# Turns of probabilities and value products, two key tiles at a time, in an attention phase on one core

## The chip, the core and the metric

The kernel runs on one core of a Trainium2 chip. The time is the device time of one execution in microseconds (us); of several runs the median is given. The core's engines run side by side, each through its own queue in program order: TensorE (PE; its weight loads are shown apart as PEld), VectorE (DVE), ScalarE (ACT), GpSimd (POOL) and SyncE (SP), which issues most of the DMAs. TensorE reads from SBUF and writes into PSUM, which is handed out here in banks of 128 partitions by 512 floats.

## The reference

One layer of a decoder: a sparse attention beside a state-space layer, then an output projection and a gated feed-forward network, for a prompt of 1024 rows and for eight short decode rows. The change is in the attention of the prompt. Its core, for one chunk of 128 queries:

```python
s_s = jnp.einsum('bqgrd,bqgkjd->bqgrkj', qg, k_sel)...      # selected blocks: all earlier keys here
p_s = masked_softmax(s_s * scale, key_pos <= q_pos)
o_s = jnp.einsum('bqgrn,bqgnd->bqgrd', p_s, v_sel)
p_w = masked_softmax(einsum(qg, kv_win[:, :, 0]) * scale, m_w)   # sliding window of 512
o_w = jnp.einsum('bqgrw,bwgd->bqgrd', p_w, kv_win[:, :, 1])
o = g[..., 0:1] * o_c + g[..., 1:2] * o_s + g[..., 2:3] * o_w
```

There are 8 query heads in 2 groups of 4; a group shares its keys and values, 64 wide. The top 16 blocks of 64 keys are all the blocks that a prompt of 1024 has, so the selected branch attends to all earlier keys.

## The kernel before

The program is recorded in Python and then ordered, engine by engine, by a scheduler that works with an estimate of times of its own; what it made is read from the order of instructions, shown below. It runs in phases: projection, decode rows with the compressed cache, prompt attention (`phase_attend`, with the state-space layer, the gating products and the second half of the decode attention put between its parts), output projection (`phase_mix`) and feed-forward.

Prompt attention takes query tiles of 128 rows in the order 4, 0, 6, 1, 7, 2, 5, 3 (`ORDER`). A tile c has two branches, `br` 0 over key tiles 0 to c and `br` 1 over at most five key tiles, and each is done in two halves `hf` of four heads. Such a half unit has two parts. `attend_scores` multiplies queries with keys into PSUM `as`, takes the maximum on VectorE and the exponential on ScalarE into `ap`, one strip of probabilities for each of four heads. `attend_values` follows one unit later (`LOOK`) and goes over the key tiles t. For each, `pv_tile` (line 1272) does three things:

- the turn: four transposes (line 1279), one for each head, of a block of 128 by 128 probabilities into one PSUM bank `pt`;
- the copy: the bank to SBUF, `pT`, alternately on ScalarE and VectorE (line 1281);
- the value product: two products (line 1283), one for each group, 64 columns of values by 256 of `pT`, adding into bank `aso`. The two write different halves of the partitions.

At the end `attend_out` copies `aso` away, transposes it and adds it to `att`. The compressed branch is done once for a query tile, with one key tile (`ac`, two steps).

The names in the trace: `as702pt` is the turn of query tile 7, branch 0, key tile 2; `as702pT` its copy; `aso<-as702pT` the product. The two halves share names. An f32 product stands as two rows of the trace, so a value product of one key tile is "x4" there and "x2" in the order.

PSUM has two banks for `pt` (`psum("psc", s=2, t=2, o=1, f=1)`, tag `t`, also used by `attend_out` and the turns of queries), one for `aso` (`o`) and two double ones for scores (`s`). `pT` has three buffers. Nothing but data, buffers and the scheduler's choice sets the order of turns and products. The helper `behind` (line 812), used in the decode part, makes the scheduler keep one instruction behind another on the same engine; it signals nothing.

Of the kernel before, what the change touches and what calls it, by code (L numbers as in the profile page):

```python
# [9 lines left out]
F32 = mybir.dt.float32  # L10
# [79 lines left out]
class Kernel:  # L90
# [1134 lines left out]
    def attend_values(self, c, br, hf, st, Ps, pc):  # L1225

        nc = self.nc
        k0, nk = self.attend_keys(c, br)
        if hf == 0:
            st["O"] = self.ps("o", f"aso{c}{br}")  # L1230
        O, att, l = st["O"], st["att"], st[br]
        g = self.gz[:, c].rearrange("p (h b) -> p b h", b=3)
        for t in range(nk):
            self.pv_tile([P[:, t * 128:t * 128 + 128] for P in Ps], self.vst[:, k0 + t, br, :], O, hf, pc, f"as{c}{br}{t}", t == 0, t == nk - 1)
        st["between"](2 * br + hf)
        if hf == 0:
            return
        nc.vector.reciprocal(l, l)
        nc.vector.tensor_tensor(l, l, g[:, 1 + br], op=ALU.mult)
        self.attend_out(O, l, att, pc, f"as{c}{br}", br == 0)  # L1240
        if br == 0:
            return
        O = self.ps("o", f"aco{c}")
        for i in range(2):
            self.pv_tile([st["pcb"][:, h, :] for h in (2 * i, 2 * i + 1, 4 + 2 * i, 5 + 2 * i)], self.vcp, O, i, pc, f"ac{c}", True, True)
        self.attend_out(O, st["lc"], att, pc, f"ac{c}", False)
        t = pc.tile([128, 512], F32, tag="aot", name=f"attq{c}")
        self.norm_rows(att.rearrange("p h d -> p (h d)"), t, 1.0, self.xc_d[c * 128:(c + 1) * 128, :512], f"attn{c}", "a")
# [20 lines left out]
            nc.vector.tensor_scalar(l, l, self.k("cmp_any"), None, op0=ALU.mult)  # L1269
        return l  # L1270

    def pv_tile(self, Ps, V, O, hf, pc, name, first, last):

        nc = self.nc
        n = Ps[0].shape[-1]
        pT = pc.tile([128, 512], F32, tag="apT", name=f"{name}pT{hf}", bufs=3)[:n]
        p = self.ps_t(f"{name}pt{hf}")[:n]
        for r in range(4):
            nc.tensor.transpose(p[:, r * 128:r * 128 + 128], Ps[r], self.ident)
        self.flip = not self.flip  # L1280
        (nc.scalar.copy if self.flip else nc.vector.tensor_copy)(pT, p)
        for g in range(2):
            nc.tensor.matmul(O[64 * g:64 * g + 64, 256 * hf:256 * hf + 256], V[:n, 64 * g:64 * g + 64], pT[:, 256 * g:256 * g + 256],  # L1283
                             start=first, stop=last)

    def attend_out(self, O, coef, att, pc, name, first):

# [618 lines left out]
```

## Time and profile before

| | us |
|---|---|
| median of 3 runs | 1836.43 (1834.63 to 1841.58) |
| the profiled execution | 1828.84 |
| its span | 1827.1 |
| TensorE busy | 1709.1 (94%) |
| TensorE's weight loads | 1439.4 (79%) |
| VectorE busy | 972.2 (53%) |
| ScalarE busy | 618.9 (34%) |
| GpSimd busy | 427.1 (23%) |

The span is the time from the first to the last instruction in the profile. Shares are averages over the phases. A row of the trace in order of time gives the start, the duration, the engine, the line and the operation; in square brackets stands how long the engine was idle ahead of it and what ended that. Durations of matmuls overlap, since they are pipelined: how long a piece really takes from TensorE is the distance from its start to the start of the next piece. The first turn of prompt attention starts at 477.3 us, the last value product at about 947 us.

### The profile page before, as it was taken

The numbers are of one execution on the slowest core, as the hardware profiler recorded it, in microseconds if no ns is written. First come the engines' busy times: TensorE is split into PE (matmuls) and PEld (weight loads), VectorE is DVE, ScalarE is ACT, GpSimd is POOL, SyncE is SP. The second block draws the span as 40 slices with busy tenths as digits, with TensorE's granted clock in tenths as the row PEclk, the third lists the DMA queues.
The fourth block names the chain that finished last, engine by engine and source line by source line (L and its number), as shares of the span: only waits on it lengthen the run. The fifth ranks groups of instructions, "written<-read, shape, count | busy, mean of one in ns | idle before, by whom it ended". The sixth has DMA issues, their size and how long they took to land.

```text
span 1827.1 us, 29355 instructions
## 1 busy us (share of the span) xinstructions
PE 1709.1 (94%) x11546; PEld 1439.4 (79%) x11546; DVE 972.2 (53%) x2330; ACT 618.9 (34%) x1247; POOL 427.1 (23%) x817
## 2 busy tenths in 40 slices
PE   6998999899796899999989989999999999999997
PEld 3898988788564665655657888998998999999996
DVE  4867647588988466566535443323333333333346
ACT  4523146455453355565433341111111111211210
POOL 2344545232015313341122210110110110110150
PEclk9999999899898999999999999999999999999999
DMA  8333243645231345413114221101201201201113
GB/s 297 105 86 106 70 152 119 219 157 193 65 112 63 71 161 195 152 61 104 55 60 138 92 93 58 58 24 50 67 24 47 70 24 47 70 24 47 53 47 141
DMA packets 132699, 172.43 MB, mean 94 GB/s; under 512 B 17176, under 2 KB 92312, under 8 KB 132304
## 3 DMA queue, kind: packets, MB, share of 16 engines
q1 hardware_dynamic: 123024, 136.62, 23.4%
q0 software_dynamic: 9408, 33.89, 5.8%
q8 instruction: 91, 1.49, 0.3%
q14 instruction: 48, 0.39, 0.1%
q10 hardware_dynamic: 128, 0.04, 0.0%
HBM read 143.88 MB, written 25.46 MB: 93 GB/s over the span
## 4 chain that ended last, share of the span: by engine, by line
PE 61%; DVE 6%; DMA 4%; ACT 2%; issue 1%; POOL 1%; SPq 1%; DVEq 0%; ACTq 0%; POOLq 0%
PE gu L1810 19%; PE dn L1853 13%; PE g L1810 5%; PE u L1810 4%; PE aso L1283 3%; PE as L1205 1%; PE as L1206 1%; SPq L1596 1%; PE acs L1258 1%; PE mx8M L1728 1%; PE mx2M L1728 1%; PE mx5M L1728 1%; PE mx0M L1728 1%; PE mx1M L1728 1%; PE mx4M L1728 1%
## 5 line engine op out<-in xcount | busy, mean ns | idle before, releaser
L1810 PE MATMUL gu<-h2h,wh 128*128 128x352 f32 x704 | 227.8, 324 | 5.0 <-ACT h2h L870 5.0
L1810 PE MATMUL gu<-h2h,wl 128*128 128x352 f32 x704 | 227.3, 323 | 0.0
L1810 PE MATMUL gu<-h2l,wh 128*128 128x352 f32 x704 | 226.8, 322 | 0.0
L1859 DVE TENSOR_TENSOR acc<-acc,dn 128x512 f32<-128x512 f32 x144 | 98.9, 687 | 229.9 <-PE dn L1853 229.9
L1818 POOL TENSOR_TENSOR al<-fa,ah 128x352 fp32r<-128x352 f32 (+1 forms) x66 | 69.6, 1054 | 414.8 <-ACT ah L1817 408.8
L1813 ACT ACTIVATE fa<-gu 128x352 f32<-128x352 f32 x44 | 20.4, 465 | 412.1 <-PE gu L1810 412.1
L1853 PE MATMUL dn<-dh,ah 128*128 128x512 f32 x352 | 140.3, 399 | 5.6 <-DVE fin L1862 5.2
L1810 PEld LDWEIGHTS gu<-h2h,wh 128*128 128x128 f32 x704 | 132.5, 188 | 7.9 <-ACT h2h L870 5.3
L1853 PE MATMUL dn<-dl,ah 128*128 128x512 f32 x352 | 138.7, 394 | 0.0
L1853 PE MATMUL dn<-dh,al 128*128 128x512 f32 x352 | 138.3, 393 | 0.0
L1810 PEld LDWEIGHTS gu<-h2l,wh 128*128 128x128 f32 x704 | 133.0, 189 | 3.8
L1810 PEld LDWEIGHTS gu<-h2h,wl 128*128 128x128 f32 x704 | 132.7, 188 | 3.1
L1816 DVE TENSOR_TENSOR fa<-fa,gu 128x352 f32<-128x352 f32 x44 | 22.9, 521 | 143.0 <-ACT fa L1813 143.0
L409 ACT CAST wh<-wr 128x1024 fp32r<-128x1024 f32 x44 | 46.0, 1048 | 151.8 <-PE g L1810 77.0
L1205 PE MATMUL as<-kst,aqA 128*128 128x320 f32 (+4 forms) x192 | 76.7, 403 | 16.2 <-ACT ap L1222 9.3
L1853 PEld LDWEIGHTS dn<-dh,ah 128*128 128x128 f32 x352 | 66.1, 188 | 24.5 <-ACT wh L409 7.5
L410 DVE TENSOR_TENSOR wl<-wr,wh 128x1024 fp32r<-128x1024 f32 x44 | 58.8, 1339 | 49.3 <-ACT wh L409 49.3
L1853 PEld LDWEIGHTS dn<-dl,ah 128*128 128x128 f32 x352 | 66.1, 188 | 15.6
L1853 PEld LDWEIGHTS dn<-dh,al 128*128 128x128 f32 x352 | 66.3, 188 | 8.1
L1222 ACT ACTIVATE ap<-as,asm 128x640 f32<-128x640 f32 (+3 forms) x64 | 55.8, 873 | 46.6 <-DVE asm L1221 31.3
L1221 DVE TENSOR_REDUCE asm<-as 128x1 f32<-128x640 f32 (+3 forms) x64 | 58.5, 918 | 20.7 <-PE as L1209 19.8
L1206 PE MATMUL as<-kst,aqB 128*128 128x320 f32 (+4 forms) x192 | 65.1, 344 | 4.7 <-ACT aqB L1168 4.7
(2137 smaller groups left out, 4667.9 us busy)
## 6 DMA issues: line engine op xcount, KB each, us to landing
wada<-in_w_ada SPq DMA_DIRECT2D x24, 1024.0 KB
wr<-in_w_ffn_gate SPq DMA_DIRECT2D x22, 512.0 KB
wr<-in_w_ffn_up SPq DMA_DIRECT2D x22, 512.0 KB
wd<-in_w_ffn_down SPq DMA_DIRECT2D x22, 512.0 KB
bx<-in_x_prompt SPq DMA_DIRECT2D x8, 512.0 KB
s_raw<-in_cache_kv_win SPq DMA_DIRECT2D x8, 512.0 KB
wor<-in_w_out SPq DMA_DIRECT2D x16, 256.0 KB
ex<-x_d SPq DMA_DIRECT2D x8, 512.0 KB
```

Of the source, the lines that this page charges most:

```text
L409: self.nc.scalar.copy(hi, raw)
L410: self.nc.vector.tensor_tensor(lo, raw, hi.bitcast(F32), op=ALU.subtract)
L1205: nc.tensor.matmul(Sv, qA[:, h, :], kk, start=True, stop=False)
L1206: nc.tensor.matmul(Sv, qB[:, h, :], kk, start=False, stop=not mt)
L1221: nc.vector.tensor_reduce(mx[:, :1], Sv, axis=ax, op=ALU.max, negate=True)
L1222: nc.scalar.activation(Pv, Sv, AF.Exp, bias=mx[:, :1], accum_out=l[:, h:h + 1])
L1283: nc.tensor.matmul(O[64 * g:64 * g + 64, 256 * hf:256 * hf + 256], V[:n, 64 * g:64 * g + 64], pT[:, 256 * g:256 * g + 256], start=first, s ...
L1728: nc.tensor.matmul(M[:P, :], X[k][b], w[:, k, c], start=m == 0, stop=m == 23)
L1810: nc.tensor.matmul(gu[i], w[:, k, :], h[:, k, 352 * n:352 * n + 352], start=m == 0, stop=m == 23)
L1818: nc.gpsimd.tensor_tensor(al[:, cols], a[:, :w], ah[:, cols].bitcast(F32), op=ALU.subtract)
L1853: nc.tensor.matmul(p, a[:, sl], w[:, c], start=m == 0, stop=m == 5)
L1859: nc.vector.tensor_tensor(o, o, p, op=ALU.add)
```

## The change

`pv_tile` becomes `pv_tiles`, which gets all key tiles of a half unit. It goes over them in groups of two. It records the turns (and copies) of a group, then the products of the group before; after the last group its products follow. With `behind`, every turn's first transpose is held behind the last instruction of the piece before it in this row, and every product likewise, so that the scheduler keeps the row: turns 0 and 1, turns 2 and 3, products 0 and 1, turns 4 and 5, products 2 and 3, and so on. Other work may still be put between. `pT` gets a fourth buffer. The compressed branch calls the new function with one key tile, twice. Everything else is the same text.

```diff
@@ -1230,8 +1230,8 @@
             st["O"] = self.ps("o", f"aso{c}{br}")
         O, att, l = st["O"], st["att"], st[br]
         g = self.gz[:, c].rearrange("p (h b) -> p b h", b=3)
-        for t in range(nk):
-            self.pv_tile([P[:, t * 128:t * 128 + 128] for P in Ps], self.vst[:, k0 + t, br, :], O, hf, pc, f"as{c}{br}{t}", t == 0, t == nk - 1)
+        self.pv_tiles([([P[:, t * 128:t * 128 + 128] for P in Ps], self.vst[:, k0 + t, br, :], f"as{c}{br}{t}", t == 0, t == nk - 1)
+                       for t in range(nk)], O, hf, pc)
         st["between"](2 * br + hf)
         if hf == 0:
             return
@@ -1242,7 +1242,7 @@
             return
         O = self.ps("o", f"aco{c}")
         for i in range(2):
-            self.pv_tile([st["pcb"][:, h, :] for h in (2 * i, 2 * i + 1, 4 + 2 * i, 5 + 2 * i)], self.vcp, O, i, pc, f"ac{c}", True, True)
+            self.pv_tiles([([st["pcb"][:, h, :] for h in (2 * i, 2 * i + 1, 4 + 2 * i, 5 + 2 * i)], self.vcp, f"ac{c}", True, True)], O, i, pc)
         self.attend_out(O, st["lc"], att, pc, f"ac{c}", False)
         t = pc.tile([128, 512], F32, tag="aot", name=f"attq{c}")
         self.norm_rows(att.rearrange("p h d -> p (h d)"), t, 1.0, self.xc_d[c * 128:(c + 1) * 128, :512], f"attn{c}", "a")
@@ -1269,19 +1269,42 @@
             nc.vector.tensor_scalar(l, l, self.k("cmp_any"), None, op0=ALU.mult)
         return l
 
-    def pv_tile(self, Ps, V, O, hf, pc, name, first, last):
-
-        nc = self.nc
+    def pv_tiles(self, tiles, O, hf, pc):
+
+
+        groups = [tiles[i:i + 2] for i in range(0, len(tiles), 2)]
+        prev, wait = None, []
+        for grp in groups + [None]:
+            if grp:
+                turned = []
+                for tile in grp:
+                    pT, ins = self.pv_turn(tile, hf, pc)
+                    prev = self.behind(prev, ins[0])
+                    prev = ins[-1]
+                    turned.append((tile, pT))
+                wait.append(turned)
+            if len(wait) > (1 if grp else 0):
+                for tile, pT in wait.pop(0):
+                    ins = self.pv_product(tile, pT, O, hf)
+                    self.behind(prev, ins[0])
+                    prev = ins[-1]
+
+    def pv_turn(self, tile, hf, pc):
+        nc = self.nc
+        Ps, _, name, _, _ = tile
         n = Ps[0].shape[-1]
-        pT = pc.tile([128, 512], F32, tag="apT", name=f"{name}pT{hf}", bufs=3)[:n]
+        pT = pc.tile([128, 512], F32, tag="apT", name=f"{name}pT{hf}", bufs=4)[:n]
         p = self.ps_t(f"{name}pt{hf}")[:n]
-        for r in range(4):
-            nc.tensor.transpose(p[:, r * 128:r * 128 + 128], Ps[r], self.ident)
+        ins = [nc.tensor.transpose(p[:, r * 128:r * 128 + 128], Ps[r], self.ident) for r in range(4)]
         self.flip = not self.flip
         (nc.scalar.copy if self.flip else nc.vector.tensor_copy)(pT, p)
-        for g in range(2):
-            nc.tensor.matmul(O[64 * g:64 * g + 64, 256 * hf:256 * hf + 256], V[:n, 64 * g:64 * g + 64], pT[:, 256 * g:256 * g + 256],
-                             start=first, stop=last)
+        return pT, ins
+
+    def pv_product(self, tile, pT, O, hf):
+        _, V, _, first, last = tile
+        n = pT.shape[0]
+        return [self.nc.tensor.matmul(O[64 * g:64 * g + 64, 256 * hf:256 * hf + 256], V[:n, 64 * g:64 * g + 64], pT[:, 256 * g:256 * g + 256],
+                                      start=first, stop=last) for g in range(2)]
 
     def attend_out(self, O, coef, att, pc, name, first):
```

The order of instructions on TensorE, at two places. In its rows a number behind `ap` stands for one strip of probabilities, one behind `pt` for one turn, and one behind `aso` for one branch of a query tile, both halves of it.

Query tile 7, branch 0, first half, in the middle of its eight key tiles, before:

```order
L1283 MATMUL aso_9510<-as703pT_9538,vst 64x256 x2
L1279 MATMUL as705pt_9557<-ident,ap_9353 128x128
L1279 MATMUL as705pt_9557<-ident,ap_9363 128x128
L1279 MATMUL as705pt_9557<-ident,ap_9373 128x128
L1279 MATMUL as705pt_9557<-ident,ap_9383 128x128
L1283 MATMUL aso_9510<-as704pT_9547,vst 64x256 x2
L1279 MATMUL as706pt_9566<-ident,ap_9353 128x128
L1279 MATMUL as706pt_9566<-ident,ap_9363 128x128
L1279 MATMUL as706pt_9566<-ident,ap_9373 128x128
L1279 MATMUL as706pt_9566<-ident,ap_9383 128x128
L238 MATMUL adaT_9934<-kc,ada_ev_9932 128x9 x4
L1283 MATMUL aso_9510<-as705pT_9556,vst 64x256 x2
```

And in the changed kernel, the pieces 0 to 5 of the same half unit:

```order
L1306 MATMUL aso_9510<-as700pT_9511,vst 64x256 x2
L1306 MATMUL aso_9510<-as701pT_9518,vst 64x256 x2
L1298 MATMUL as704pt_9544<-ident,ap_9353 128x128
L1298 MATMUL as704pt_9544<-ident,ap_9363 128x128
L1298 MATMUL as704pt_9544<-ident,ap_9373 128x128
L1298 MATMUL as704pt_9544<-ident,ap_9383 128x128
L1298 MATMUL as705pt_9551<-ident,ap_9353 128x128
L1298 MATMUL as705pt_9551<-ident,ap_9363 128x128
L1298 MATMUL as705pt_9551<-ident,ap_9373 128x128
L1298 MATMUL as705pt_9551<-ident,ap_9383 128x128
L1306 MATMUL aso_9510<-as702pT_9525,vst 64x256 x2
L1306 MATMUL aso_9510<-as703pT_9532,vst 64x256 x2
```

Turns and products alternate before, with an `ada` product of another part among them; now two products, two turns and two products stand together.

Query tile 2, branch 0, three key tiles, from its first turn into the second half, before:

```order
L1279 MATMUL as200pt_10370<-ident,ap_10089 128x128 x2
L1279 MATMUL as200pt_10370<-ident,ap_10101 128x128 x2
L1283 MATMUL aso_10368<-as200pT_10369,vst 64x256 x2
L1279 MATMUL as201pt_10379<-ident,ap_10089 128x128 x2
L1279 MATMUL as201pt_10379<-ident,ap_10101 128x128 x2
L1279 MATMUL as202pt_10388<-ident,ap_10089 128x128 x2
L1279 MATMUL as202pt_10388<-ident,ap_10101 128x128 x2
L1283 MATMUL aso_10368<-as201pT_10378,vst 64x256 x2
L1279 MATMUL as200pt_10462<-ident,ap_10346 128x128 x2
L1279 MATMUL as200pt_10462<-ident,ap_10358 128x128 x2
L1283 MATMUL aso_10368<-as202pT_10387,vst 64x256 x2
```

And in the changed kernel:

```order
L1298 MATMUL as200pt_10370<-ident,ap_10089 128x128 x2
L1298 MATMUL as200pt_10370<-ident,ap_10101 128x128 x2
L1298 MATMUL as201pt_10377<-ident,ap_10089 128x128 x2
L1298 MATMUL as201pt_10377<-ident,ap_10101 128x128 x2
L1298 MATMUL as202pt_10384<-ident,ap_10089 128x128 x2
L1298 MATMUL as202pt_10384<-ident,ap_10101 128x128 x2
L1306 MATMUL aso_10368<-as200pT_10369,vst 64x256 x2
L1306 MATMUL aso_10368<-as201pT_10376,vst 64x256 x2
L1298 MATMUL as200pt_10462<-ident,ap_10346 128x128 x2
L1298 MATMUL as200pt_10462<-ident,ap_10358 128x128 x2
L1306 MATMUL aso_10368<-as202pT_10383,vst 64x256 x2
```

Before, the first product stands behind the first turn; now the third turn stands there, and the first two products come behind it. Over the whole phase, counted in the order, value products stand in 132 unbroken runs before and in 97 in the changed kernel.

## Rows read from the trace of the kernel before

**Rows 1.** The page: span; busy time, share and instructions of TensorE.

```profile
span 1827.1 us, 29355 instructions
...
PE 1709.1 (94%) x11546; PEld 1439.4 (79%) x11546; DVE 972.2 (53%) x2330; ACT 618.9 (34%) x1247; POOL 427.1 (23%) x817
```

**Rows 2.** Windows: stretch, length, busy PE, PEld, DVE, ACT, POOL; clock; DMA share, GB/s.

```profile
475.00:667.00 192.00, 161.83 (x1534) 112.34 (x1534) 143.53 (x411) 87.83 (x214) 56.96 (x79) 0.91 0.32 95
667.00:947.00 280.00, 263.05 (x1719) 164.84 (x1717) 167.21 (x266) 154.95 (x348) 74.47 (x259) 1.00 0.31 106
800.00:840.00 40.00, 32.81 (x217) 21.83 (x217) 31.39 (x49) 29.59 (x64) 14.76 (x42) 1.00 0.39 129
947.00:1827.00 880.00, 859.74 (x4768) 783.95 (x4768) 326.39 (x439) 165.32 (x281) 121.32 (x218) 1.00 0.20 62
```

**Rows 3.** TensorE's waits, 475 to 947: who, for whom; us, times, longest.

```profile
PE as L1205 <- ACT ap L1222: 9.3, 6, 5.6
...
PE aco L1283 <- DVE ac0pT L1281: 4.4, 1, 4.4
```

**Rows 4.** TensorE in order of time, query tile 7: start us, us, instruction.

```profile
735.15 0.65 PE L1283 MATMUL aso<-as701pT,vst 128*64 128x256 f32 x4
735.73 0.66 PE L1279 MATMUL as703pt<-ident,ap 128*128 128x128 f32 x4
736.31 0.65 PE L1283 MATMUL aso<-as702pT,vst 128*64 128x256 f32 x4
736.90 0.66 PE L1279 MATMUL as704pt<-ident,ap 128*128 128x128 f32 x4
```

**Rows 5.** The same, query tile 5.

```profile
851.41 0.65 PE L1283 MATMUL aso<-as501pT,vst 128*64 128x256 f32 x4
851.89 0.60 PE L1283 MATMUL aso<-as502pT,vst 128*64 128x256 f32 x4
852.43 0.66 PE L1279 MATMUL as503pt<-ident,ap 128*128 128x128 f32 x4
852.92 0.60 PE L1279 MATMUL as504pt<-ident,ap 128*128 128x128 f32 x4
```

**Rows 6.** The same, query tile 4.

```profile
523.14 0.60 PE L839 MATMUL s111pt<-ident,s_S 128*128 128x128 f32 x4
523.67 0.65 PE L1283 MATMUL aso<-as413pT,vst 128*64 128x256 f32 x4
```

**Rows 7.** Line 1279, weight loads: count, ns min/median/max, first and last start.

```profile
L1279 PEld LDWEIGHTS as402pt<-ident,ap x8: 138/140/143, 487.4 to 504.9; 128*128 128x128 f32 x8
```

**Rows 8.** TensorE's waits, 667 to 947; eight of aso, first and last.

```profile
PE mn7t L862 <- DMA mn7xn<-xn_d: 1.9, 1, 1.9
...
PE aso L1283 <- ACT as210pT L1281: 0.8, 1, 0.8
...
PE aso L1283 <- DVE as313pT L1281: 0.3, 1, 0.3
```

**Rows 9.** TensorE in order of time, query tile 2.

```profile
810.26 0.60 PE L1279 MATMUL as200pt<-ident,ap 128*128 128x128 f32 x4
811.54 0.65 PE L1283 MATMUL aso<-as200pT,vst 128*64 128x256 f32 x4 [0.68 <-ACT as200pT L1281]
```

**Rows 10.** Line 1281, copies: count, ns min/median/max.

```profile
L1281 ACT COPY as500pT<-as500pt x2: 586/587/588, 843.5 to 860.2; 128x512 f32<-128x512 f32 x2
L1281 DVE COPY as501pT<-as501pt x2: 683/688/692, 846.0 to 860.8; 128x512 f32<-128x512 f32 x2
```

**Rows 11.** TensorE in order of time, query tile 2, second branch.

```profile
830.00 0.61 PE L1279 MATMUL as210pt<-ident,ap 128*128 128x128 f32 x4
830.44 0.60 PE L1279 MATMUL as211pt<-ident,ap 128*128 128x128 f32 x4
831.77 0.66 PE L1279 MATMUL as212pt<-ident,ap 128*128 128x128 f32 x4 [0.73 <-ACT as211pT L1281]
```

## The prediction

> **What bounds the kernel now.** I read the page's first lines, then busy time by stretch, then TensorE's waits, then single turns and products in order of time. TensorE (PE) is busy for 94% of a span of 1827.1 us [rows 1]. The changed code runs between about 475 and 947 us. Three stretches behave differently [rows 2]. From 475 to 667 us TensorE is busy 161.8 of 192 us with VectorE (DVE) at 143.5, and its long waits end on other engines (9.3 us on `ap`, ScalarE's exponentials; 4.4 us on a copy queued on DVE) [rows 3]: time saved on TensorE there mostly becomes a longer wait. From 667 to 947 us it is busy 263.1 of 280 us at full clock, and from 947 to the end 859.7 of 880. So a microsecond saved on TensorE after 667 us moves everything behind it, nearly in full. That is where I count.
>
> **What the change removes.** No instruction goes and none is added: 4 transposes (a turn) and 2 products for each of 148 tile steps, and 148 copies, stay. What changes is who stands next to whom. Where turns and products alternate, each takes 0.58 or 0.59 us from its start to the next one's start, so a tile costs 1.17 us [rows 4]. Where two products follow each other, the first takes 0.48 and the second 0.54; of two turns behind a product the first takes 0.49 [rows 5]; a turn behind a turn and ahead of a product takes 0.53 [rows 6]. Two tiles alternating: 4 x 0.585 = 2.34 us. Two turns, then two products: 0.49 + 0.53 + 0.48 + 0.54 = 2.04 us. So each merged pair saves 0.30 us of TensorE without any wait going away: the price of passing between 128 columns (turns) and 64 columns (products). The least a merger can save is the products' side alone, 1.17 - 1.02 = 0.15 us, where other work parts the turns.
>
> How many mergers there are is told by the order. Products stood in 132 unbroken runs and stand in 97: 35 fewer. By query tile in the order of work: 4: 21 to 15, 0: 5 to 5, 6: 23 to 19, 1: 10 to 8, 7: 26 to 19, 2: 11 to 9, 5: 21 to 15, 3: 15 to 7. Tiles 1, 7, 2, 5 and 3 run after 667 us: 25 mergers. Products followed directly by a turn fall from 109 to 53, so mostly both sides merge, and I take 0.30: 25 x 0.30 = 7.5 us (at 0.15: 3.8). Of the ten mergers in tiles 4 and 6 (3.0 us) the waits of the first stretch swallow most; I keep 0.6, bounds 0 and 3.0.
>
> [...] The rows show four weight loads of 140 ns each [rows 7] in a turn that gives way to the next turn after 0.49 us, less than 4 x 0.14 = 0.56, so loads run beside the matmuls of the same rows. [...]
>
> **The waits on copies.** Before, a product could meet its own copy only one turn later. After 667 us eight such waits, from 0.8 down to 0.3 us, add to 4.2 us [rows 8]. In the changed order two or three turns or products stand between a turn and its product where a tile has three key tiles or more, so 1.45 us or more pass from the turn's start (0.49 + 2 x 0.48), against 1.28 us from a turn's start to its product's when nothing stands between [rows 9]; so these waits go. (The 16 steps of the compressed branch stay alone, turn then product.) What is late next is the PSUM bank: there are two `t` banks, and the third turn needs the first one's copied out. A ScalarE copy takes 0.59 us, a DVE copy 0.69 [rows 10]. At the start of query tile 2 by hand: turn 0 at 0, turn 1 at 0.44 as two turns in a row stand in [rows 11], turn 2 when bank 0 is free at 1.28, so 0.35 to 0.4 us idle where 0.68 [rows 9] and then 0.3 were; no more in that half. Tile 3 has four key tiles: turn 2 waits 0.4, turn 3 another 0.1 to 0.45, which is about as much as it loses. With 4.2 us of waits going and bank waits of 0.4 to 0.9 us in the four half units of tiles 2 and 3 that start bare (2.6 us at the middle), I take a gain of 1.6 us; bounds 4.2 gained and 3.0 lost. Tiles 7 and 5 have scores and other fillers between their turns; there I take a loss of 1.0 us for bank waits (bounds 0 and 2), since pairs of copies now ask for ScalarE and DVE together, behind exponentials and maxima.
>
> **The rest.** The edges join instructions of one queue, so no semaphore is added. The fourth `pT` buffer takes space, no time. The scheduler moves other things too: stores of `att` and norm chains on SP and POOL by a few places, ada and glu products by a few on PE. Of these only the mix transposes `mn7t` wait for a DMA, 1.9 us [rows 8]; they now stand one turn later, so up to 1.9 us could be gained, or as much lost if the row's store before it issues later on SP. I take 0. The chain of edges also holds a second tile's four transposes behind the first tile's fourth, which waits for the last head's exponential; before, both tiles' transposes of a ready head went ahead between scores. What stands behind them on PE are scores of the next unit; the work is the same, so I take 0, with at most a turn (0.49 us) lost at such a place in the first stretch.
>
> **Sum.** 7.5 + 0.6 + 1.6 - 1.0 = 8.7 us less. The profiled execution took 1828.8 us (span 1827.1), 7.6 us under the median of the runs, 1836.4; the sum on it is 1820.1, and on the median 1827.7. I forecast 1828, its own range 1823 to 1833: at worst 25 x 0.15 + 1.6 - 2.0 = 3.4 us gained, at best 7.5 + 3.0 + 4.2 - 1.0 = 13.7. A measurement of this kernel tells a change from none at about 0.5%, 9.2 us: 1827.2 is the border, just beyond my number.
>
> **Rivals.**
> [...]
> - *All is gained*: all 35 mergers at 0.30 (10.5 us), the 4.2 us of waits and the DMA's 1.9 count in full: 1836.4 - 16.6 = 1820. For it: in the first stretch, too, turns end later chains. Against: VectorE's 143.5 of 192 there.
> - *Slower: the bank waits win.* One mechanism: with turns in pairs a third turn meets two full banks. Its price is in the trace: of three turns in a row, at 830.00 and 830.44, the third waits 0.73 us for a copy [rows 11]. There are 32 half units (8 query tiles, 2 branches, 2 halves). It decides from (10.5 + 9.2) / 32 = 0.6 us a half unit on; at 0.73 in all of them 23.4 - 10.5 = 12.9 us slower, 1849. Against: scores, glu or ada products lie between most turns of tiles 4 to 7, so the banks are emptied beside them.
> [...]
>
> **Chances.** The forecast 0.50 (0.18 of it below the border), all gained 0.22, nothing gained 0.18, bank waits 0.08, clock 0.02. Faster by over 0.5%: 0.18 + 0.22 = 0.40. Within: 0.32 + 0.18 + 0.02 (weak bank waits) = 0.52. Slower: 0.08. Likeliest is a gain of about 8 us, near the border. The range 1819 to 1841 takes in the cases of no gain and nearly all of full gain, and leaves out the slower rivals.
>
> **What would show it.** Right: rows of products in pairs with strides near 0.48 and 0.54, turns at 0.49 and 0.53; the stretch from tile 1's turns to the last product shorter by 7 to 9 us with TensorE's busy time there falling by about as much; waits of `aso` on copies nearly gone, a few on `pt` tiles of 0.3 to 0.5 us in their place; the stretch behind it unchanged at about 880 us. Wrong: strides of 0.58 within pairs (the price isn't the passage); `pt` waits adding to more than 10 us; the first stretch longer or shorter by over 4 us; or a granted clock under 1.00 after 667 us.

## The result and the profile after

The changed kernel takes 1844.5 us (median of 18 runs, 1837.8 to 1854.3) where the kernel before, beside it, takes 1835.2 (18 runs): ratio 1.0051, 95% interval 1.0036 to 1.0066. It is slower by half a per cent, 9.3 us. The forecast was 1828 us and the range ended at 1841. One run of all in this document, of e_ones, took 2869.6 us at a clock of 0.66; it was in a slow state, and its row below is from the other eleven.

The profiled executions lie on opposite sides of these medians (before 6.4 us under, after 9.0 over), so their spans differ by more than the kernels do: by 24.6 us, of which 4.8 lie ahead of prompt attention. I therefore use two numbers over all runs as well: the mean granted clock of TensorE, and span x mean clock, an estimate of the time that would be left with the clock full throughout (it counts the whole span as if it stretched with the clock). The page of after, to set beside [rows 1]; of its table of slices the row of TensorE's clock in tenths, 46 us a slice:

```profile
span 1851.7 us, 29350 instructions
...
PE 1730.2 (93%) x11546; PEld 1460.6 (79%) x11546; DVE 974.1 (53%) x2330; ACT 618.8 (33%) x1247; POOL 424.3 (23%) x817
...
PEclk9999999999797899998999999999999999999999
```

The same instructions keep TensorE busy 21 us longer, at a mean clock of 0.967 in this execution (before's: 0.979). Windows of after, columns as in [rows 2]; the first is tile 1's first turn to the last product:

```profile
702.00:971.00 269.00, 246.41 (x1565) 156.82 (x1563) 156.03 (x240) 143.29 (x314) 64.15 (x235) 0.96 0.30 99
866.00:876.00 10.00, 9.58 (x42) 5.25 (x42) 2.62 (x6) 3.63 (x9) 3.41 (x15) 0.50 0.39 132
957.00:961.00 4.00, 4.00 (x24) 3.15 (x24) 1.99 (x4) 1.40 (x3) 0.00 (x0) 0.62 0.65 232
971.00:1851.00 880.00, 862.63 (x4768) 786.23 (x4768) 325.78 (x438) 165.25 (x281) 121.28 (x217) 0.99 0.19 62
```

The first of these stretches, in before:

```profile
687.00:947.00 260.00, 243.05 (x1578) 151.42 (x1576) 152.96 (x240) 143.18 (x314) 67.66 (x235) 1.00 0.31 104
```

The stretch that was to be 7 to 9 us shorter is 9 us longer (269.7 against 260.7, from turn to product), although the twelve products of one GLU tile have left it, and the clock, 1.00 before, is 0.96 in it: (1 - 0.96) x 269 = 10.8 us. The part of attention ahead of it, tiles 4, 0 and 6, is 10.0 us longer too (219.4 against 209.4), at a clock of 0.88 against 0.92. For ten microseconds from 866 on the clock is 0.50 ("half clock" below). The tail is unchanged. TensorE's waits on turns (`pt`) and products (`aso`) in this stretch of after, columns as in [rows 3]:

```profile
PE as503pt L1298 <- ACT as502pT L1300: 2.5, 1, 2.5
PE as212pt L1298 <- ACT as211pT L1300: 2.1, 1, 2.1
...
PE aso L1306 <- DVE as101pT L1300: 0.9, 1, 0.9
PE as501pt L1298 <- ACT as500pT L1300: 0.7, 1, 0.7
...
PE aso L1306 <- DVE as111pT L1300: 0.2, 1, 0.2
```

Waits ahead of turns add to 8.1 us (before 2.2); two make up 4.6 of them. Waits ahead of products are 4.3 us (before 4.4). So waits for banks came, and waits for copies did not go.

The new order itself costs what was predicted. TensorE in order of time, tile 7, after:

```profile
744.90 0.65 PE L1306 MATMUL aso<-as700pT,vst 128*64 128x256 f32 x4
745.38 0.60 PE L1306 MATMUL aso<-as701pT,vst 128*64 128x256 f32 x4
745.91 0.66 PE L1298 MATMUL as704pt<-ident,ap 128*128 128x128 f32 x4
746.40 0.60 PE L1298 MATMUL as705pt<-ident,ap 128*128 128x128 f32 x4
746.93 0.65 PE L1306 MATMUL aso<-as702pT,vst 128*64 128x256 f32 x4
```

From start to start 0.48, 0.53, 0.49, 0.53 us, as in [rows 5, 6]: 2.03 us for two tiles against 2.34 [rows 4].

Now the head of tile 5, where the larger wait stands. TensorE in order of time, after:

```profile
861.48 0.60 PE L1298 MATMUL as500pt<-ident,ap 128*128 128x128 f32 x4
862.81 0.66 PE L1298 MATMUL as501pt<-ident,ap 128*128 128x128 f32 x4 [0.73 <-ACT as500pT L1300]
863.31 0.60 PE L1298 MATMUL as502pt<-ident,ap 128*128 128x128 f32 x4
866.42 1.11 PE L1298 MATMUL as503pt<-ident,ap 128*128 128x128 f32 x4 [2.51 <-ACT as502pT L1300]
867.46 1.12 PE L1306 MATMUL aso<-as500pT,vst 128*64 128x256 f32 x4
868.37 1.07 PE L1306 MATMUL aso<-as501pT,vst 128*64 128x256 f32 x4
```

ScalarE in the same microseconds:

```profile
861.38 0.72 ACT L1069 ACTIVATE woh<-wor,vecs 128x512 fp32r<-128x512 f32 x1 [0.45 <-DMA wor<-in_w_out]
862.17 0.58 ACT L1300 COPY as500pT<-as500pt 128x512 f32<-128x512 f32 x1
862.78 0.72 ACT L1069 ACTIVATE woh<-wor,vecs 128x512 fp32r<-128x512 f32 x1
865.17 0.72 ACT L1069 ACTIVATE woh<-wor,vecs 128x512 fp32r<-128x512 f32 x1 [1.67 <-DMA wor<-in_w_out]
865.80 0.56 ACT L1300 COPY as502pT<-as502pt 128x512 f32<-128x512 f32 x1
```

Four turns stand in a row for two banks. The copy that frees a bank takes 0.56 us, but in ScalarE's queue it stands behind a piece of the output weights (`woh`, line 1069) that waits 1.67 us for its own load. TensorE stands still for 2.51 us, and behind that a turn or product takes 0.91 to 1.04 us from start to start instead of about half.

Why are the weights there? Their pool opens when the last tile of the gating products (GLU), `gl3`, is done. The last operation of `gl3`, then the pieces of weights on ScalarE (count, ns min/median/max, first and last start), in before:

```profile
811.76 0.69 POOL L1133 TENSOR_SCALAR gl3s<-gl3s,gl3n_y 128x512 f32<-128x512 f32 x1
L1069 ACT ACTIVATE woh<-wor,vecs x16: 710/722/725, 816.8 to 839.9; 128x512 fp32r<-128x512 f32 x16
```

And in after:

```profile
834.55 0.69 POOL L1133 TENSOR_SCALAR gl3s<-gl3s,gl3n_y 128x512 f32<-128x512 f32 x1
L1069 ACT ACTIVATE woh<-wor,vecs x16: 712/722/724, 839.2 to 865.2; 128x512 fp32r<-128x512 f32 x16
```

In before this operation starts 1.5 us behind tile 2's first turn (810.26 [rows 9]), and the pieces end ahead of tile 5's first turn (842.86). After, it starts 8.3 us behind tile 2's first turn (826.23), and the pieces run into the head of tile 5, whose first turn is at 861.48. In before's order 22 products with the weights (`mx8M`, of the output projection) stood behind the turn of as502, ahead of the next product and the turn of as503, as cover:

```profile
845.79 0.60 PE L1279 MATMUL as502pt<-ident,ap 128*128 128x128 f32 x4
846.14 0.48 PE L1728 MATMUL mx8M<-woh,mx8Xh 128*32 128x512 f32 x1
```

### The profile page after: what moved, and what is told of

Its sections match the earlier page's. It is cut to its first block, busy times and chain, and to the rows that moved or that the text cites. A ratio compares the mean times of both kernels' runs of the same rounds, so it can differ in the third digit from the quotient of the medians.

```text
span 1851.7 us, 29350 instructions
## 1 busy us (share of the span) xinstructions
PE 1730.2 (93%) x11546; PEld 1460.6 (79%) x11546; DVE 974.1 (53%) x2330; ACT 618.8 (33%) x1247; POOL 424.3 (23%) x817
## 4 chain that ended last, share of the span: by engine, by line
PE 62%; DVE 6%; DMA 4%; ACT 2%; issue 1%; POOL 1%; SPq 1%; ACTq 0%; POOLq 0%; DVEq 0%
PE gu L1833 18%; PE dn L1876 13%; PE g L1833 5%; PE u L1833 4%; PE aso L1306 3%; PE as L1205 2%; PE as L1206 1%; PE mx7M L1751 1%; PE mx8M L1751 1%; PE mx5M L1751 1%; PE Y L1636 1%; PE mx2M L1751 1%; PE mx0M L1751 1%; PE mx1M L1751 1%; PE mx4M L1751 1%
## 5 line engine op out<-in xcount | busy, mean ns | idle before, releaser
L1876 PEld LDWEIGHTS dn<-dl,ah 128*128 128x128 f32 x352 | 66.7, 189 | 15.8
```

What stands on the lines that cost most here:

```text
L1876: nc.tensor.matmul(p, a[:, sl], w[:, c], start=m == 0, stop=m == 5)
```

## The experiments

Theories. *Clock*: the held order makes TensorE stand still among turns, the granted clock falls behind it, and that is the loss. *Waits*: the bank waits cost the time by themselves. *Displacement* (formed after the first four runs): the change pushes GLU tiles and weights to a place where they block the copies. The table has all runs; each group of rows shared a chip and its runs of before, which stand in its first row. "Full-clock time" is the mean of span x mean clock of each run (standard error 0.6 to 2.0 us).

| kernel | us, before | us, this | ratio (95%) | clock, before / this | full-clock us, before / this |
|---|---|---|---|---|---|
| after (first) | 1835.2 | 1844.5 | 1.0051 (1.0036-1.0066) | - / .9716 | - / 1790.9 |
| e_buf4 | 1832.7 | 1835.7 | 1.0012 (0.9999-1.0026) | .9763 / .9742 | 1788.5 / 1787.1 |
| e_noedges | | 1839.6 | 1.0042 (1.0028-1.0057) | / .9731 | / 1790.4 |
| e_ones | | 1840.7 | 1.0032 (1.0017-1.0047) | / .9763 | / 1794.6 |
| e_wopool | | 1844.4 | 1.0052 (1.0038-1.0066) | / .9718 | / 1791.4 |
| e_after2 | 1825.6 | 1835.9 | 1.0059 (1.0039-1.0080) | .9784 / .9728 | 1784.6 / 1783.3 |
| e_busy | | 1842.1 | 1.0097 (1.0074-1.0120) | / .9735 | / 1791.6 |
| e_gle | | 1825.2 | 1.0001 (0.9986-1.0015) | / .9758 | / 1779.1 |
| e_gleB | | 1829.9 | 1.0027 (1.0007-1.0047) | / .9773 | / 1787.8 |
| e_gle2 | 1825.9 | 1823.9 | 0.9992 (0.9977-1.0006) | .9780 / .9752 | 1784.2 / 1777.5 |
| e_glne | | 1827.1 | 1.0008 (0.9994-1.0021) | / .9769 | / 1783.2 |
| e_glx3 | | 1826.9 | 1.0016 (1.0000-1.0033) | / .9740 | / 1778.4 |
| e_glx23 | | 1834.4 | 1.0050 (1.0032-1.0067) | / .9745 | / 1785.6 |
| e_glx046 | 1825.7 | 1819.6 | 0.9964 (0.9941-0.9986) | .9788 / .9787 | 1785.2 / 1778.3 |
| e_gla | | 1830.7 | 1.0027 (1.0009-1.0046) | / .9745 | / 1782.8 |
| e_x046 | 1825.6 | 1827.2 | 1.0004 (0.9989-1.0020) | .9793 / .9781 | 1786.1 / 1785.1 |
| e_glx046b | | 1815.9 | 0.9949 (0.9931-0.9968) | / .9789 | / 1776.5 |

**The fourth buffer alone** (before, `bufs=3` to `bufs=4`; every engine's order is before's).

> The kernel before with a fourth buffer for the turned tiles and nothing else; every engine's order of instructions is before's. Clock theory (the held order makes TensorE stand still among turns, and it is the granted clock that then costs the time): time as before, 1835 us, within 2 us of it; mean granted clock over its runs .976 to .979 against .972 for the changed kernel, and time x clock about 1790 us in both. Wait theory (the waits for banks cost the time by themselves, the clock differs by chance): mean clock about .972 as in the changed kernel, and time x clock some 9 us lower than there. Buffer theory (the fourth buffer, by where it puts things, costs something): 1840 us or more.

It is before within the interval; the buffer is not the cause. Its clock, .974, lies between the two kernels, so some of a clock difference of .002 is chance. Its trace shows how much one trace can differ: with before's order the stretch from tile 1 on has a clock of 0.98, with 10.2 us at half clock where before's trace has none, though not at tile 5's head. Windows of e_buf4:

```profile
690.00:955.00 265.00, 247.65 (x1585) 154.31 (x1583) 153.58 (x242) 142.81 (x315) 67.52 (x235) 0.98 0.30 103
```

**No edges** (after without the two `behind` lines in `pv_tiles`).

> The changed kernel recorded in twos, without the order-only edges: 120 runs of products instead of 97 (before 132), 38 product-to-turn changes instead of 25 (before 82). Clock theory: the scheduler may again put score and MLP products where a turn would wait, so most of the stalls at the head of a value pass go and the clock comes back to about .975: 1835 to 1838 us. Recording-order theory (it is the order in which turns and products are recorded that costs, not the holding): as the changed kernel, 1842 to 1847 us.

At 1.0042 it is as slow as the changed kernel within the intervals: recording in twos moves the same GLU products and puts the same two waits there (1.9 and 1.6 us). So the loss does not need the held order.

**One tile at a time, held** (`groups = [[tile] for tile in tiles]`).

> The changed kernel's edges, with groups of one tile: T0 T1 P0 T2 P1 ..., so 138 runs of products: nothing of the gain from merged products (7.5 us by the prediction), but the holding. Clock theory and wait theory both: as slow as the changed kernel or slower, 1844 to 1852 us, with the clock at .972 or lower under the clock theory. If instead two tiles at a time are what hurts (two full banks at the third turn), 1835 to 1838 us.

Slower than before by 0.32%, but by another road than either theory said: the clock is before's, and full-clock time is 6 us up, with only 4.2 us of waits ahead of turns in the same stretch. So holding single tiles costs something too, in work and waits and not in clock.

**Output weights on GpSimd** (lines 1069 and 1070 become three GpSimd operations).

> The changed kernel with the preparation of the output weights (woh and wol, 16 pieces, 840 to 870 us) moved from ScalarE and VectorE to GpSimd, so that no copy out of a turn's bank stands behind a piece whose load has not landed. In the changed kernel such copies ended the 2.09 us wait at 845.8 us and the 2.51 us wait at 863.9 us, and the clock fell right behind both. Clock theory: both waits shrink under 0.8 us, no half-clock window begins between 840 and 880 us, and the time falls by the waits (3 us) and half of 13.6 us, to about 1835 us (a round of chance of 3 us). Wait theory: by the 3 to 4 us of the waits alone, 1840 us. If neither place matters: 1844 us.

The wait of as503 fell to 0.3 us, that of as212 is gone, and no half clock begins between 840 and 880 us, where after's begins at 848.7 and 865.8, as the clock theory said; the total did not move. GpSimd, busy 127.0 us from tile 1 to the last product (after: 64.2), is slower at it: the last piece starts at 916.9 us (after: 865.2), so the products that use the weights leave tile 5, and tile 3 waits 7.1 us for banks and has ten microseconds at 0.51 (922 to 932) instead. The loss only changes place. Windows of e_wopool, last product to the first down product (182 us where after has 151), columns as above:

```profile
938.00:1120.00 182.00, 163.91 (x847) 140.47 (x846) 78.40 (x120) 61.63 (x119) 37.37 (x158) 0.94 0.34 110
```

The total says nothing on the cause: the experiment brought a cost of its own.

**Fillers in the waits.**

```diff
+    FILL = {"as4110": 7, "as7021": 6, "as2111": 8, "as5000": 2, "as5020": 9}
...
                     prev = ins[-1]
+                    for _ in range(self.FILL.get(f"{tile[2]}{hf}", 0)):
+                        mm = self.nc.tensor.matmul(O[0:64, 256 * hf:256 * hf + 256], self.vst[:, 0, 0, 0:64], ..., start=True, stop=True)
+                        prev = self.behind(prev, mm)
```

> The changed kernel with 32 filler products (128x64 by 128x256 f32, about 0.24 us each by the product rows, results overwritten) that stand where TensorE stood still in the changed kernel's trace: 7 behind the turn as411 (2.08 us), 6 behind as702 (1.58 us), 8 behind as211 (2.09 us), 2 behind as500 (0.73 us), 9 behind as502 (2.51 us). The order at these places is the changed kernel's with the fillers put in. Clock theory (standing still among turns at these places lets the granted clock fall): no half-clock window within 5 us behind 845, 863 and 761 us, mean clock over the runs back from .972 to .975 or more, time 1836 to 1839 us although 7.7 us of work is added. Wait theory (the waits cost by themselves, the clock is chance): clock stays .972, and the time is the changed kernel's or up to 2 us more, 1844 to 1847 us.

At tile 5's head it did what the clock theory said. TensorE in order of time, e_busy:

```profile
860.00 0.60 PE L1303 MATMUL as502pt<-ident,ap 128*128 128x128 f32 x4
860.53 4.10 PE L1287 MATMUL aso<-vst 128*64 128x256 f32 x18
864.57 0.43 PE L1744 MATMUL mx8xt<-ident,mx8xc 32*128 32x32 f32 x4
864.93 0.66 PE L1303 MATMUL as503pt<-ident,ap 128*128 128x128 f32 x4
```

The window behind it:

```profile
864.00:874.00 10.00, 10.00 (x62) 5.58 (x61) 2.04 (x5) 2.73 (x6) 1.97 (x8) 1.00 0.12 43
```

The turn comes even later (4.9 us behind that of as502, in after 3.1), but nothing idles and the clock stays at 1.00. In total it lost 6 us over e_after2, but the expectation had the size of the fillers wrong: the nine above take 4.04 us from start to start, and all 32 take 14.6 us, 0.46 each and not 0.24, in place of 9.0 us of waits. The difference, 5.6 us, is about the loss. The mean clock is only .9735 against .9728: the stretch from tile 1 on is at 0.99 (e_after2 0.97), but tile 6, where no filler stands and other products changed places, had 31.8 us at half clock in its trace (e_after2 15.8, after 25.5). So the fall at this place goes when products stand in the gap. It isn't shown whether it takes the standing still alone or also the lack of products: in after TensorE had nothing but transposes from 861.0 to 867.5 us. Nor is it shown whether fillers of the right size would pay.

**The changed kernel again.**

> The changed kernel again, for a second trace and for times beside the other three on one chip. Clock theory: half-clock windows again behind the bank waits at the heads of as21 and as50 and none of them in tiles 1 and 7 of before; mean clock .971 to .973, 1842 to 1846 us. If the windows of the first trace were chance: other places, and the sum of half clock between tile 1 and the last product within 7 us of before's (0).

The second trace repeats the first: waits of 2.34 and 1.5 us at the same heads, half clock behind the longer one. Window behind as503 in e_after2:

```profile
846.00:856.00 10.00, 8.89 (x38) 4.95 (x38) 3.40 (x8) 4.32 (x10) 3.41 (x15) 0.52 0.41 133
```

Over its runs the clock costs (1 - .9728) x 1834.9 = 49.9 us, before's (1 - .9784) x 1825.8 = 39.4: 10.5 of a mean difference of 9.1. Full-clock time is 1.3 us lower, which is within its error.

**GLU tiles earlier**, in the changed kernel (e_gle, e_gle2), and the same table in before (e_gleB). The table says behind which half unit of a query tile a piece of other work is recorded; a G with a number is a GLU tile.

```diff
-1: ('', '', '', ''), 7: ('G6 T6 T7 G0', 'G1 T9', 'T10', 'G2 T8 G5'), 2: ('T11', 'G4 G3', '', '')
+1: ('', '', '', 'G6'), 7: ('T6 T7 G0', 'G1 T9 G2', 'T10 G5', 'G4 T8 G3'), 2: ('T11', '', '', '')
```

> The changed kernel with the GLU tiles recorded a pass or more earlier (only the table of the interleaved work changes). In the changed kernel the last GLU tile ended at 834.5 us, 8 us behind the start of tile 2, where before it had ended 2 us ahead of it; so the output weights came 10 us later against the attention, and their pieces stood before the copies as211pT and as502pT on ScalarE and VectorE. With this table the pieces stand on ScalarE where they stood before the change, with products still in pairs (94 runs). Displacement theory: the waits of 2.09 us (as212) and 2.51 us (as503) go, the falls behind them (13.6 us at half clock) too, and the merged products' 7 us show: 1829 to 1834 us. If the displaced GLU tile is not the cause: 1842 to 1846 us.

> The same table of interleaved work put into the kernel before, without pairs: control for the run above. Both theories: within 3 us of before (about 1833 to 1836 us). If it gains as much as the run above does against the changed kernel, the table itself is what helps, whatever the products' order.

> The changed kernel with the earlier GLU tiles (as e_gle), on another chip. Displacement theory: level with before or faster, ratio .996 to 1.001; no half-clock window between tile 1's first turn and the head of tile 3 (in e_gle: none); the part of the time that is not clock (time x clock) 4 to 6 us under before's. If e_gle's 5 us of unclocked gain was chance: ratio 1.003 or more.

Without pairs the table costs 0.27%; with pairs it brings the changed kernel from 1.0059 to 1.0001, and to 0.9992 on another chip. By the means of the runs pairs are 6 us better than singles with this table, and 9 us worse with the old one; at full clock, with this table, 8.7 us better. Tile 5's head in e_gle, TensorE in order of time:

```profile
840.86 0.61 PE L1298 MATMUL as501pt<-ident,ap 128*128 128x128 f32 x4
841.30 0.60 PE L1298 MATMUL as502pt<-ident,ap 128*128 128x128 f32 x4
841.66 0.47 PE L1751 MATMUL mx8M<-woh,mx8Xh 128*32 128x512 f32 x1
```

The window from tile 1 to the last product, e_gle:

```profile
686.00:939.00 253.00, 233.77 (x1570) 152.52 (x1568) 154.67 (x240) 142.86 (x314) 66.10 (x235) 1.00 0.31 105
```

The weights are ready (`mx8M` uses them already), the products that covered the place in before are back, and the clock is 1.00. As times both expected ranges missed, since before is 10 us faster here than on the chip that they were written for. Set against the kernels beside them, e_gle gained 10.7 us on the changed kernel where 8 to 17 were expected, and e_gleB lost 4.3 us where at most 3 were. The expectation's "2 us ahead" for `gl3` in before is misread (it is 1.5 us behind); in e_gle it is 0.3 behind. e_gle still has a lower clock than before (.9758 and .9752 against .978).

**Its edges off, and single tiles taken out.**

> e_gle without the order-only edges: the table with earlier GLU tiles and tiles recorded in twos; 119 runs of products against e_gle's 94, 42 changes from product to turn against 25. If the edges are what merges the products and merging is worth the 0.30 us of the prediction: 25 runs more, so 5 to 7 us of work more, 1.003 to 1.004 of before. If the recording order alone does it: level with e_gle.

> e_gle with tile 3, the last and short one, left as before (recorded one tile at a time, no edges); 102 runs of products. In e_gle's trace the waits for banks that were left lay in tile 3 (0.7 and 0.7 us) and the half clock from tile 3's head to the first down product was 17.1 us against 6.8 before. Clock theory: that falls to about 7 us, and with 8 merged runs fewer (2.4 us) the time is 2 to 3 us under e_gle: .997 to .999 of before. If those windows are chance: 0 to 3 us over e_gle.

> As e_glx3, with tile 2 left as before too (106 runs of products): the waits of 1.2 and 0.7 us for as212's bank in e_gle go, 4 merged runs (1.2 us) are lost. Both theories: within 2 us of e_glx3; under it if the wait of as212 costs more than the merged products of tile 2 give.

e_glne: the edges are worth 5.7 us of full-clock time, as expected, but 3 of these go again in clock (.9752 with, .9769 without): 1.0008 instead of the 1.003 expected, against 0.9992 with them, a difference inside the intervals. In the stretch from tile 1 on e_glne has 73 runs of products to e_gle's 55, and TensorE is busy 241.8 us against 234.0 (some 3 us of it by half clock), but it waits only 14.3 us against 18.5: in these two traces most of what the mergers save there comes back as waits. e_glx3 came out as expected for the case that tile 3's half clock was chance (3 us over e_gle2 by the means). e_glx23 missed by far: tile 2 takes 42.6 us instead of 31.9; why is open.

**Half the cure, and pairs only where TensorE is the bound.** e_gla records only the last GLU tiles earlier. The others leave tiles 4, 0 and 6 as before:

```diff
     def pv_tiles(self, tiles, O, hf, pc):
+        c = int(tiles[0][2][2])
+        if c in (0, 4, 6):
+            for tile in tiles:
+                pT, _ = self.pv_turn(tile, hf, pc)
+                self.pv_product(tile, pT, O, hf)
+            return
```

with the earlier GLU tiles (e_glx046) and with the old table (e_x046).

> The changed kernel with only the last two GLU tiles recorded a pass earlier: on ScalarE no piece of the output weights stands any more between as500pT and as502pT, but six still stand right before as211pT. Displacement theory: the wait of as503 (2.5 and 2.3 us in the two traces of the changed kernel) and the 10.2 us of half clock behind it go, the wait of as212 (2.1 and 1.5 us) stays: about 2.4 + 5.1 = 7 us under the changed kernel, .999 to 1.003 of before. If the fall behind as503 comes whatever waits there: 1.005 or more, and a half-clock window at tile 5's head.

> e_gle (pairs held, GLU tiles earlier) with tiles 4, 0 and 6 left as before (one tile at a time, no edges); 106 runs of products instead of 94. In those tiles TensorE waits for other engines anyway; e_gle's two traces show 16.6 and 20.3 us at half clock in tile 6 against 13.0 in before, and mean clocks of .975 against .978. If the pairs there cost clock: tile 6 back to 13 us, mean clock .977, 3 to 4 us under e_gle: .996 to .998 of before. If the half clock there is chance: 12 merged runs (3.6 us) lost in part behind waits, 0 to 3 us over e_gle.

> The changed kernel with tiles 4, 0 and 6 left as before and the old table of interleaved work; 107 runs of products. On TensorE the GLU products stand between the turns as in before, but on ScalarE the pieces of the output weights stand where the changed kernel has them (six before as211pT, two between as500pT and as502pT). If the place of these pieces is what makes the waits: as212 and as503 wait 1.5 us or more again, half clock of 10 us behind as503, and the time is 8 to 12 us over e_glx046: 1.001 to 1.004 of before. If it was the displaced GLU products (12 to tile 6, 12 to tile 7) that made the loss: level with e_glx046, .995 to .998.

> e_glx046 again beside it, on another chip: .994 to .999 of before if its gain is real, mean clock within .001 of before's and time x clock 5 to 8 us under before's; 1.000 or more if it was chance.

e_gla: as503 no longer waits, the head of tile 5 (847 to 864 us) is at a clock of 1.00 and the tile 8.0 us shorter than in after (73.4 against 81.3), and the ratio is 1.0027, in the range expected. The wait of as212, which was to stay, is only 0.7 us; tile 2 fell to a clock of 0.55 (826 to 837 us) all the same, behind a wait of 2.66 us on `aqB` (queries, copied by ScalarE), not on a bank.

e_x046 has the GLU products in the query tiles where before has them, and yet `gl3` ends 8.3 us behind tile 2's first turn. Tile 5's head is the changed kernel's to the hundredth:

```profile
842.79 0.60 PE L1304 MATMUL as502pt<-ident,ap 128*128 128x128 f32 x4
845.90 1.11 PE L1304 MATMUL as503pt<-ident,ap 128*128 128x128 f32 x4 [2.51 <-ACT as502pT L1306]
```

The window behind it:

```profile
845.00:855.00 10.00, 9.10 (x40) 5.06 (x42) 3.06 (x7) 4.11 (x10) 3.41 (x15) 0.50 0.40 132
```

e_glx046b beside it, the window of the same place and that from tile 1 to the last product:

```profile
842.00:852.00 10.00, 10.00 (x73) 6.73 (x72) 3.62 (x7) 3.03 (x7) 2.04 (x8) 1.00 0.07 27
...
681.00:934.00 253.00, 236.85 (x1580) 154.78 (x1578) 154.63 (x242) 143.19 (x314) 67.39 (x235) 0.99 0.32 107
```

Tile 5 takes 81.1 us in e_x046 and 71.2 in e_glx046b; the means are 10.2 us apart, where 8 to 12 were expected. At this head it is the place of the weights, not the displaced GLU products, that costs. e_x046's ratio, 1.0004, came out under the range expected. e_glx046 is faster than before in both sets of runs, 0.9964 and 0.9949, which shared a chip, though the second was meant for another. The expectation that its clock would be before's held (.9787 and .9789 against .9788 and .9793).

Set side by side, each against its own before: pairs everywhere, 1.0059 with the old table and 1.0001 and 0.9992 with the earlier GLU tiles; pairs only from tile 1 on, 1.0004 and 0.9964 and 0.9949. Either remedy alone takes the loss away, and only both together gain. The first part of attention shows the second one: in the six traces without pairs there (before, e_buf4, e_gleB, e_x046, both of e_glx046) its clock is 0.91 to 0.93, in the eight with them and without fillers (after, e_after2, e_wopool, e_gle, e_gle2, e_gla, e_glx3, e_glx23) 0.88 to 0.92, mostly 0.90.

## Why the prediction was wrong

By the runs of e_after2 the sum missed by 17.8 us: 8.7 less were forecast, 9.1 more came. At full clock only 1.3 of the 8.7 us were gained, so 7.4 are missing there, most of them waits (item 2); the other 10.5 are clock, for which the sum had nothing.

1. *25 mergers x 0.30 us = 7.5 us: right as a price.* The strides are as read; which part of passing from turn to product takes the time, no run shows. Where little else interferes (e_glx046b), the stretch from tile 1 to the last product, with the same work in it, is 253.4 us against 260.7, 7.3 us shorter, with 26 runs of products fewer and waits of 15.4 us in all against 16.3; in the other trace of that kernel it is 6.4 us shorter. Over all runs full-clock time falls by 6.9 and 9.6 us. That the order is worth nothing is refuted by these runs.
2. *Waits on copies, 4.2 us gone, 2.6 + 1.0 us of bank waits come: this step failed.* Together a gain of 0.6 us was forecast; in after 0.1 us of the first went and 5.9 us of the second came, a loss of 5.8. I priced a bank by an idle engine's copy (0.59 and 0.69 us [rows 10]) and gave tiles 7 and 5 "scores and other fillers between their turns". Tile 5's head had no filler left, and the copies stood behind pieces of weights that waited for DMAs. The rival "bank waits win" had the mechanism, but spread it evenly, 0.73 us [rows 11] in 32 half units; in truth two places of 32 hold 4.6 of the 8.1 us. The sum's worst case, 3.4 us gained, also kept the first term at its middle: at its own bounds (3.0 lost, 0 in the first stretch) it is 1.2 us lost.
3. *"The scheduler moves other things too ... I take 0": failed.* Two of the GLU tiles' products left tile 1, `gl3` ended 6.8 us later against tile 2, and the weights came into the two heads. Undoing that alone (e_gle) takes the loss away. It is not the only root: in e_x046 it stays, with the wait of 2.51 us, and the loss is gone too. Why the scheduler puts `gl3`'s end later even where the products stay (e_x046) was not settled.
4. *First stretch, 0.6 us gained, bounds 0 and 3.0: failed.* Pairs in tiles 4, 0 and 6 cost more than they give: leaving them out takes 7 us or so off e_gle (about 0.4%, across chips) and brings the mean clock from about .9755 to .9788 (two sets of runs each). What stands ahead of the half clock there was not traced.
5. *The clock, 0.02: badly weighed.* The chance was an estimate of mine. In before's trace TensorE is busy 32.8 of the 40 us from 800 on at a clock of 1.00 [rows 2], but that is one stretch of one trace. The runs show falls behind gaps. Three of three traces with a wait of 2.3 to 2.5 us at tile 5's head (after, e_after2, e_x046) show 0.50 to 0.52 behind it; e_gle, e_busy, e_gla and e_glx046b, without the wait, show 1.00 there. Over the runs of e_after2 the price is 10.5 us.

## What to carry to other kernels

Price a wait for a buffer not by the copy that frees it but by what stands ahead of that copy in its engine's queue, and look there for instructions that wait for a DMA. When a change shifts a scheduled order, follow what opens or frees something later (here a pool of weights) and ask where its work lands now; and keep cover at places where TensorE would idle, since here a gap of 2.5 us was followed by 10.2 us at half clock, some 5 us more. A change in one part can undo a gain in another, so take it out part by part.

## What the runs showed of the hardware

A gap of 2.3 to 2.5 us of TensorE among turns was followed by about 10 us at half clock (0.50, 0.52 and 0.50 in after, e_after2 and e_x046), some 5 us of time, in each of three traces. A shorter one at the same place did not show it: 1.6 us in e_noedges, where a product stood among the turns, with no half clock in tile 5 and a clock of 0.99 from tile 1 to the last product. The same kind of gap is not always followed by the fall: `mn7t`'s wait of 1.9 us in before [rows 8] left the clock at 1.00 [rows 2], with products on both sides of `mn7t`; the same wait of 1.96 us in after, between turns alone, was followed by 0.62 (957 to 961 us, above). Even with an identical order the mean clock of one set of runs was .976 and of another .974 (before and e_buf4), 4 us of time. Two products of one key tile, which write different halves of the partitions, took 0.48 to 0.58 us together in tiles 7 and 5, and 0.43 and 0.44 in tile 3 of after, where four stand in a row; fillers of the same size that all wrote the same half took 0.46 us each (e_busy).
